# Second layer's FFN: six groups of four blocks by seven products, with the sums of their weights made in HBM by GpSimd's transfers

## The chip, the cores and the metric

One core of a Trainium2 chip runs the whole program. The engines of a core run side by side, each in its own order, and wait for each other through semaphores: TensorE (PE; PEld is its loading of stationary tiles) multiplies, VectorE (DVE) and ScalarE (ACT) work element by element, GpSimd (POOL) does the little that is left, and SyncE (SP) issues the transfers of weights from HBM. The metric is the device time of one execution in microseconds, lower being better; the median of three runs before the change is 2675.32 us.

## What is computed

The program is a decoder trunk of two layers over 256 tokens of width 2048, in float32. The first layer has multi-head latent attention, the second a dilated attention in three groups; behind each stands the same feed-forward network (FFN), whose up-projection has 2 x 5632 columns (a gate half and a value half) and whose down-projection has 5632 rows:

```python
def conv_ffn(h, w_up, conv_w, conv_b, w_down):
    u = h @ w_up
    up = jnp.pad(u, ((0, 0), (CONV_WIDTH - 1, 0), (0, 0)))
    c = conv_b + up[:, 0:S] * conv_w[0]
    for j in range(1, CONV_WIDTH):
        c = c + up[:, j:j + S] * conv_w[j]
    gate, val = c[..., :FFN_HIDDEN], c[..., FFN_HIDDEN:]
    return (jax.nn.silu(gate) * val) @ w_down

for i in range(DEPTH):
    h = rms_norm(x, attn_norm[i])
    ...
    h = rms_norm(x, ffn_norm[i])
    x = x + conv_ffn(h, ffn_w_up[i], ffn_conv_w[i], ffn_conv_b[i], ffn_w_down[i])
return rms_norm(x, final_norm)
```

## The kernel before

**Precision.** A weight tile w that has arrived from HBM is split into a high part wh (ScalarE, the line `nc.scalar.activation(h, w[:, c:e], AF.Copy)` of `load`, L91) and a remainder wl = w - wh (VectorE, L92). The activations are kept as such pairs too (`xs`, `a`). A product is then high by high, high by low and low by high; low by low is left out.

**A unit.** The ordinary product, `proj` (L137), makes one block of 128 output columns for all 256 tokens. The weight block is stationary. For each of the 16 chunks of the 2048 rows, wh meets 512 columns (the tokens' high and low parts side by side) and wl meets 256. An up-projection of one FFN block takes two such units, gate and value (`up`); there are 44 blocks. `keep` then multiplies by the norm's factors (L972), and `conv` does the convolution, the SiLU and the product of the halves (L958 to L967) and leaves the pair `a` for the down-projection. `down` runs 16 chunks of output columns over 10 to 12 finished blocks at a time; the bank of PSUM is first seeded with the residual (L120).

**A four by seven products.** In each layer three groups of four blocks (`SEVEN = (12, 23, 34)`) are done in another way, `seven`: tokens, rows and the two halves gate and value are each cut in two, and seven products take the place of eight, as in Strassen's scheme. Here the tokens' forms are stationary (128 columns) and the weights of four blocks move: each of the seven products has 8 steps of three matmuls of 512 columns (L853 to L855), 168 matmuls for a four. The forms of the tokens (s1 to s4) are made once by `make_forms` (L820 to L827). Four of the seven products need sums of weight blocks, which VectorE makes on the chip from tiles that have arrived (L881, L892, L893) before they are split. When all products are there, `sums` and `last_sum` add them up, `turn` transposes the result back with TensorE (L947, 16 matmuls for a four), and `conv` reads it from PSUM.

**Order.** A scheduler lays out each engine's instructions from the order of the code. Six of a four's products ride between the chunks of a `down` (`mains`), the seventh (`thirds`) and the turns between later units (`steps`). Weights stream through three tiles `w` (pool `wst`) and five tiles each of wh and wl (pool `wsp`), so a load waits until the tile three loads back has been split, and a split until TensorE has used the piece five pieces back. GpSimd's part is small: constants, the zero columns of `upad` (L802) and the reciprocal square roots of the norms (L309), one small instruction at the start of each stage, on which TensorE's instruction that spreads the result (`spread`, L296) waits.

## Time and profile before

| what | value |
|---|---|
| median of three runs (range) | 2675.32 us (2675.04 to 2677.12) |
| span of the profiled execution | 2673.9 us, 1.4 us under that median; the rest lies around the span |
| TensorE's first matmuls of the second FFN | 1938.4 us |
| TensorE's last matmul of the second FFN's last `down` | 2661 us |
| bytes read from HBM | 501.50 MB, 188 GB/s over the span |

In the rows of the profile a line is that of the kernel, an arrow points from what is read to what is written, and x384 counts instructions. In a timeline the first two numbers are the start in the span and the length in microseconds; since matmuls are pipelined, the cost of a run of matmuls is read from the start of the next one, not from the length. A row of a table by windows gives, for a stretch of the span, its length and then how many microseconds of it each engine was busy, the granted clock (1.00 is full), the share of time that the 16 DMA engines were busy, and GB/s.

### The profile page before, as it was taken

To read this page: it belongs to the slowest core of one execution; us is meant where nothing else is said; L and a number is where in the kernel's file an instruction comes from. 1 tells how busy PE (TensorE), PEld (TensorE's weight loads), DVE (VectorE), ACT (ScalarE), POOL (GpSimd) and SP (SyncE) were. 2 spreads that over 40 slices of the span, in tenths; PEclk is the share of its full clock that TensorE was granted. 3 is DMA by queue.
4 is the path that set the end of the run, shared out by engine and by line. 5 is a ranking of instruction groups with operands and counts; after the bars stand their busy time and mean duration, and the time that the engine had idled before them with its cause. 6 is when DMAs were issued, how large, how long until landed. Compare 5 with 4: busy or idle time off the path is not lost.

```text
span 2673.9 us, 40017 instructions
## 1 busy us (share of the span) xinstructions
PE 2657.8 (99%) x15167; PEld 2338.4 (87%) x15167; DVE 2105.5 (79%) x3630; ACT 1639.7 (61%) x2624; POOL 24.7 (1%) x39
## 2 busy tenths in 40 slices
PE   9999999999999999999999999999999999999998
PEld 7998888888888888898888888888888888888887
DVE  7987888898898876676577667667688889889885
ACT  6775666676666764444454444445666667666665
POOL 2000000000000000000000000000000000000000
PEclk9999999999999999999999999999999999999999
DMA  6335555656566565544544544544555575755744
GB/s 246 138 133 203 189 182 193 239 179 224 197 202 227 182 206 198 179 171 170 191 170 164 197 161 174 188 174 160 189 189 175 191 249 171 223 205 189 237 169 147
DMA packets 153553, 506.19 MB, mean 189 GB/s; under 512 B 11024, under 2 KB 86160, under 8 KB 118928
## 3 DMA queue, kind: packets, MB, share of 16 engines
q1 hardware_dynamic: 153072, 503.46, 54.9%
q8 instruction: 119, 1.95, 0.3%
q14 instruction: 74, 0.61, 0.1%
q10 hardware_dynamic: 288, 0.18, 0.0%
HBM read 501.50 MB, written 2.10 MB: 188 GB/s over the span
## 4 chain that ended last, share of the span: by engine, by line
PE 95%; DMA 1%; DVE 1%; issue 0%; ACT 0%; SPq 0%; DVEq 0%; ACTq 0%
PE pp L137 70%; PE pp L165 3%; PE pp L167 3%; PE pp L166 3%; PE ps L855 1%; PE ps L853 1%; PE ps L854 1%; DMA w<-in_wup 1%; PE pp L104 1%; PE pp L106 1%; PE pp L105 1%; PE pp L853 1%; PE pp L854 1%; PE pp L855 1%; PE po L781 1%; PE ps L744 1%
## 5 line engine op out<-in xcount | busy, mean ns | idle before, releaser
L92 DVE TENSOR_TENSOR wl<-w,wh 128x1024 fp32r<-128x1024 f32 (+3 forms) x802 | 881.9, 1110 | 371.0 <-ACT wh L91 228.1
L91 ACT ACTIVATE wh<-w 128x1024 fp32r<-128x1024 f32 (+3 forms) x802 | 770.9, 966 | 370.8 <-PE pp L137 220.7
L137 PE MATMUL pp<-xs,wh 128*128 128x512 f32 x3648 | 855.5, 390 | 0.0
L137 PEld LDWEIGHTS pp<-xs,wh 128*128 128x128 f32 x3648 | 677.1, 188 | 135.8 <-DVE xs L266 0.2
L137 PE MATMUL pp<-xs,wl 128*128 128x256 f32 x3648 | 465.3, 284 | 0.0
L137 PEld LDWEIGHTS pp<-xs,wl 128*128 128x128 f32 x3648 | 455.7, 191 | 9.3
L137 PE MATMUL pp<-a,wh 128*128 128x512 f32 x1920 | 459.7, 390 | 0.0
L137 PEld LDWEIGHTS pp<-a,wh 128*128 128x128 f32 x1920 | 357.7, 188 | 72.6
L137 PEld LDWEIGHTS pp<-a,wl 128*128 128x128 f32 x1920 | 248.1, 191 | 10.2
L137 PE MATMUL pp<-a,wl 128*128 128x256 f32 x1920 | 252.8, 283 | 0.0
L155 DVE TENSOR_TENSOR wl<-w,wh 128x1024 fp32r<-128x1024 f32 x96 | 116.2, 1218 | 62.3 <-ACT wh L154 50.3
L154 ACT ACTIVATE wh<-w 128x1024 fp32r<-128x1024 f32 x96 | 101.6, 1059 | 96.5 <-PE pp L166 50.0
L213 ACT ACTIVATE lo<-pp 128x256 f32<-128x256 f32 x225 | 85.7, 381 | 119.5 <-PE pp L137 119.4
L165 PE MATMUL pp<-wh,xs 128*128 128x512 f32 x384 | 150.0, 391 | 0.0
L167 PE MATMUL pp<-wl,xs 128*128 128x512 f32 x384 | 149.5, 389 | 0.0
L166 PE MATMUL pp<-wh,xs 128*128 128x512 f32 x384 | 149.4, 389 | 0.0
L962 DVE SCALAR_TENSOR_TENSOR cv<-upad,convs,cv 128x256 f32<-128x256 f32 x256 | 121.1, 481 | 18.3 <-ACT cv L958 15.9
L958 ACT ACTIVATE cv<-upad,convs 128x256 f32<-128x256 f32 x128 | 76.4, 598 | 72.7 <-DVE upad L972 71.0
L215 DVE TENSOR_TENSOR sum<-pp,lo 128x256 f32<-128x256 f32 x225 | 94.1, 418 | 0.2
L120 ACT ACTIVATE pp<-x 128x512 f32<-128x512 f32 x144 | 85.1, 591 | 13.6 <-DVE sum L215 6.8
L880 ACT ACTIVATE wh<-w 128x1024 fp32r<-128x1024 f32 x48 | 51.0, 1062 | 60.0 <-PE pp L137 43.0
L167 PEld LDWEIGHTS pp<-wl,xs 128*128 128x128 f32 x384 | 72.1, 188 | 15.0
(299 smaller groups left out, 3154.7 us busy)
## 6 DMA issues: line engine op xcount, KB each, us to landing
w<-in_wup SPq DMA_DIRECT2D x128, 1024.0 KB, 4.8
w<-in_win SPq DMA_DIRECT2D x96, 1024.0 KB, 4.8
w<-in_wup SPq DMA_DIRECT2D x96, 512.0 KB, 5.1
w<-in_win SPq DMA_DIRECT2D x96, 512.0 KB, 4.1
w<-in_wdn SPq DMA_DIRECT2D x64, 704.0 KB, 4.1
w<-in_wdn SPq DMA_DIRECT2D x32, 768.0 KB, 4.2
w<-in_wdn SPq DMA_DIRECT2D x32, 640.0 KB, 5.3
w<-in_wo SPq DMA_DIRECT2D x16, 1024.0 KB, 4.7
```

Source lines behind the costliest of these rows:

```text
L91: nc.scalar.activation(h, w[:, c:e], AF.Copy)
L92: nc.vector.tensor_sub(l, w[:, c:e], h.bitcast(F32))
L120: nc.scalar.activation(dst, chunk.unsqueeze(1).to_broadcast([P, 2, 2, P]), AF.Copy, scale=0.5)
L137: nc.tensor.matmul(ps[:, i * T:], w_k, xs[k][:, :(2 - i) * T], start=(k == 0 and i == own), stop=(k == n - 1), skip_group_check=(i != own))
L154: nc.scalar.activation(wh4, src, AF.Copy)
L155: nc.vector.tensor_sub(wl4, src, wh4.bitcast(F32))
L165: nc.tensor.matmul(ps, xh, wh, start=k == 0, stop=False)
L166: nc.tensor.matmul(ps, xl, wh, start=False, stop=False)
L167: nc.tensor.matmul(ps, xh, wl, start=False, stop=k == KC - 1)
L213: nc.scalar.activation(t, ps[:, T:], AF.Copy)
L215: nc.vector.tensor_add(u, ps[:, :T], t)
L962: nc.vector.scalar_tensor_tensor(o, v, convs[:, cw + j:cw + j + 1], o, op0=ALU.mult, op1=ALU.add)
```

## The change

The first layer keeps its code. The second layer's FFN, now `ffn_ahead`, does six fours by seven products instead of three, and so 20 blocks by ordinary units instead of 32. The sums of weights are no longer made on the chip: `plan_sums` lays out, for each of the six fours, four sums t1 to t4 in HBM, each by a plain copy of a weight block (96 transfers of 512 KB) and transfers that add another block or sum to it in place (96 more). They stand on GpSimd's queue. `some_ahead`, called by every `load` from the ninth on, issues the next copy and the add that is six steps older on two of five loads, and ties both to the last high split that was recorded (`state["split"]`), so that they aren't issued ahead of it. There are 102 steps. The weight of each of the seven products is now loaded as two tiles of 1 MB in rows of 2 KB, from the weights or from the sums, and split like any other. Rows are halved as first half and second half (before: even and odd chunks). The products of a four come one by one (1, 2, 6, 7, 4, 5, 3), each into a bank of pool `pss`, and `use` adds each up as it is done. `PERIODS` and the calls of `deal` and `put` place these half products and the turns behind single units and single chunks of `down`.

```diff
+FIRST = 12
+PERIODS = ((0, 11, 12, 16, (20, 21, 22)), (11, 22, 23, 27, (31, 32, 33)), (22, 33, 34, 38, (42, 43)))
...
+            some_ahead()
...
-                        nc.scalar.activation(h, w[:, c:e], AF.Copy)
+                        state["split"] = nc.scalar.activation(h, w[:, c:e], AF.Copy)
...
+        ahead = []
+        made = {}
+        def plan_sums(layer, fours):
+            copies, adds = [], []
+            for fb0 in fours:
+                t = {i: hbm.tile([4, P, WS], F32, name=f"t{i}_{layer}_{fb0}") for i in (1, 2, 3, 4)}
+                made[layer, fb0] = t
+                last = None
+                for f in range(4):
+                    blk = lambda h, j: wup_d[layer, 2 * (fb0 + f) + h, :, j * WS:(j + 1) * WS]
+                    copies += [(t[i][f], blk(*hj)) for i, hj in ((1, (0, 0)), (3, (1, 1)), (2, (1, 1)), (4, (0, 1)))]
+                    adds += [(t[1][f], blk(1, 0)), (t[3][f], blk(1, 0)), (t[2][f], t[1][f])]
+                    if last:
+                        adds.append(last)
+                    last = (t[4][f], t[2][f])
+                adds.append(last)
+            late = 6
+            for n in range(len(copies) + late):
+                ahead.append((copies[n] if n < len(copies) else None, adds[n - late] if n >= late else None))
+        def some_ahead():
+            state["loads"] = state.get("loads", 0) + 1
+            if state["loads"] > 8 and state["loads"] % 5 in (0, 3) and ahead:
+                c, a = ahead.pop(0)
+                made_by = []
+                if c:
+                    made_by.append(nc.gpsimd.dma_start(*c))
+                if a:
+                    made_by.append(nc.gpsimd.dma_start(*a, accum_op=ALU.add, max_dma_last_dim=WS))
+                for i in made_by:
+                    tc.add_manual_dep(i.ins, state["split"].ins.name, mybir.DependencyInfo(
+                        mybir.DependencyClass.Sync, mybir.DependencyReason.SCHED_ONLY), reason="pace")
...
+        def ffn_ahead(layer, goff, ready):
...
+            products = {1: ("a11", (0, 0)), 2: ("a12", (0, 1)), 3: ("s4", (1, 1)), 4: ("a22", 4), 5: ("s1", 1),
+                        6: ("s2", 2), 7: ("s3", 3)}
+            def seven(fb0):
+                t = made[layer, fb0]
+                ps = {}
+                u = {}
+                quarters = {}
+                def product(i, q):
+                    name, what = products[i]
+                    if q == 0:
+                        ps[i] = pss.tile([P, 512], F32, name="ps", tag="ps")
+                    w = wst.tile([P, D], F32, name="w", tag="w")
+                    if isinstance(what, int):
+                        src = t[what][:, :, q * HALF:(q + 1) * HALF]
+                    else:
+                        h, j = what
+                        src = wup_d[layer, 2 * fb0:2 * fb0 + 8].rearrange("(f i) p c -> i f p c", i=2)[h]
+                        src = src[:, :, j * WS + q * HALF:j * WS + (q + 1) * HALF]
+                    nc.sync.dma_start(w.rearrange("p (f c) -> p f c", f=4), src.rearrange("f p c -> p f c"))
+                    w5 = w.rearrange("p (f k c) -> p k f c", f=4, k=4)
+                    for h in range(2):
+                        wh = wsp.tile([P, WS], F32R, name="wh", tag="wh")
+                        wl = wsp.tile([P, WS], F32R, name="wl", tag="wl")
+                        as4 = lambda t: t.rearrange("p (k f c) -> p k f c", k=2, f=4)
+                        nc.scalar.activation(as4(wh), w5[:, 2 * h:2 * h + 2], AF.Copy)
+                        nc.vector.tensor_sub(as4(wl), w5[:, 2 * h:2 * h + 2], as4(wh).bitcast(F32))
+                        for k in range(2):
+                            kk = 4 * q + 2 * h + k
+                            xh, xl = stationary(name, kk)
+                            bh, bl = wh[:, ts(k, HALF)], wl[:, ts(k, HALF)]
+                            nc.tensor.matmul(ps[i], xh, bh, start=(kk == 0), stop=False)
+                            nc.tensor.matmul(ps[i], xl, bh, start=False, stop=False)
+                            nc.tensor.matmul(ps[i], xh, bl, start=False, stop=(kk == KC // 2 - 1))
+                    if q == 1:
+                        sums.append(lambda: use(i))
...
+                out = []
+                for i in (1, 2, 6, 7, 4, 5, 3):
+                    for q in range(2):
+                        out.append(lambda i=i, q=q: (product(i, q), None if q == 1 else settle()))
+                return out, settle, [lambda f=f: turn(f) for f in range(4)]
...
+            first = [[] for _ in range(2 * FIRST)]
+            downs = [[[] for _ in range(KC)] for _ in PERIODS]
+            ups = [[[] for _ in range(2 * len(p[-1]))] for p in PERIODS]
+            def put(rows, at, *moves):
+                rows[at].extend(moves)
+            def deal(moves, rows, counts):
+                for row, n in zip(rows, counts):
+                    row.extend(moves[:n])
+                    del moves[:n]
+            for s, (a, b, one, two, singles) in enumerate(PERIODS):
+                m, settle, turns = seven(one)
+                if s == 0:
+                    deal(m, first[12:], [1] * 12)
+                    deal(m, downs[0], (1, 1))
+                else:
+                    put(ups[s - 1], 0, m.pop(0))
+                    put(ups[s - 1], 1, m.pop(0))
+                    deal(m, ups[s - 1][4:], (2, 2))
+                    deal(m, downs[s], (2, 2, 2, 2))
+                m, settle2, turns2 = seven(two)
+                put(downs[s], 4, settle, m.pop(0))
+                put(downs[s], 5, m.pop(0))
+                put(downs[s], 6, *turns[:2])
+                put(downs[s], 7, *turns[2:])
+                deal(m, downs[s][8:], (1, 2, 1, 2, 1, 2, 1, 2))
+                ups[s][0].insert(0, settle2)
+                ups[s][2] += turns2[:2]
+                put(ups[s], 3, *turns2[2:3])
+                if len(ups[s]) > 4:
+                    put(ups[s], 4, *turns2[3:])
+                else:
+                    put(ups[s], 3, *turns2[3:])
+            slots = first
+            for fb in range(FIRST):
+                up(fb)
+            for (a, b, _, _, singles), d, u in zip(PERIODS, downs, ups):
+                slots = d
+                down(a, b)
+                slots = u
+                for fb in singles:
+                    up(fb)
+            flush()
+            down(PERIODS[-1][1], FB, True)
+            flush()
...
+        plan_sums(1, [fb for _, _, one, two, _ in PERIODS for fb in (one, two)])
...
-            ffn(1, G_FFN + KC, final)
+            ffn_ahead(1, G_FFN + KC, final)
```

Counted over the program, TensorE loses 384 matmuls of 512 columns and 384 of 256 from its units, and gains 504 of 512 columns in the sevens and 48 transposes.

Three places show how the order stands. First GpSimd's queue, with the reciprocal square roots (`rcol<-ms,negh`; the one of row 20 belongs to the first FFN). Before, only the zeroing of `upad` stood ahead of it:

```order
13 L309 TENSOR_TENSOR rcol<-ms,negh 128x2 [waits DVE_49]
14 L321 TENSOR_TENSOR s_546<-ms,negh 128x2 [waits DVE_49]
15 L321 TENSOR_TENSOR s_759<-ms,negh 128x2 [waits DVE_49]
16 L802 MEMSET upad_3600 128x2 [waits DMAHW6_49,PE_49,Activation_49]
...
20 L309 TENSOR_TENSOR rcol<-ms,negh 128x2 [waits DVE_49] x2
```

Now it stands in the row of transfers. `t_1_12_122` is sum t4 of the four that begins at block 12 (119 to 122 are t1 to t4), a row from `in_wup` at L224 is a copy, a row at L226 an add; the names behind "waits" are semaphores: DMASW of earlier transfers of this queue, Activation of ScalarE, DVE of VectorE.

```order
36 L224 DMA t_1_12_122<-in_wup 128x1024 [waits DMASW0_49,Activation_49]
37 L226 DMA t_1_12_120<-t_1_12_119 512x256 [waits DMASW5_49,DMASW1_49]
38 L224 DMA t_1_12_119<-in_wup 128x1024 [waits DMASW2_49,Activation_49]
39 L226 DMA t_1_12_122<-t_1_12_120 512x256 [waits DMASW3_49]
40 L348 TENSOR_TENSOR rcol<-ms,negh 128x2 [waits DVE_49]
41 L224 DMA t_1_12_121<-in_wup 128x1024 [waits DMASW4_49,Activation_49]
42 L226 DMA t_1_12_119<-in_wup 128x4x256
43 L224 DMA t_1_12_120<-in_wup 128x1024 [waits DMASW6_49,Activation_49]
```

The square root now has four transfers ahead of it that belong to the same few loads, and two of these wait for earlier transfers.

Second, TensorE's rows around the turns of a four that is finished inside a `down` (L961 are the transposes, to the banks `pt` and `po`; L141 with `a` are the chunks of `down`, 11 blocks each; L915 to L917 are the sevens):

```order
9299 L141 MATMUL pp<-a,wh 128x512 x11
9300 L141 MATMUL pp<-a,wl 128x256 x11
9301 L961 MATMUL pt<-cst,t_21020 128x128 x2
9302 L961 MATMUL pt<-cst,t_21019 128x128 x2
9303 L961 MATMUL po<-cst,t_21020 128x128 x2
9304 L961 MATMUL po<-cst,t_21019 128x128 x2
9305 L141 MATMUL pp<-a,wh 128x512 x11
9306 L141 MATMUL pp<-a,wl 128x256 x11
9307 L141 MATMUL pp<-a,wh 128x512 x2
9308 L961 MATMUL pt<-cst,t_21020 128x128 x2
9309 L961 MATMUL pt<-cst,t_21019 128x128 x2
9310 L141 MATMUL pp<-a,wh 128x512 x9
```

Between the first pair of turns and the second stand one chunk and a piece of the next, and the fourth turn follows the first matmul of a seven, two rows below the last one shown. Before, a pair of turns stood inside an ordinary unit (here the second pair of the third four; L137 with `xs`):

```order
10900 L137 MATMUL pp<-xs_19795,wl 128x256
10901 L947 MATMUL pt<-cst,t_25705 128x128 x2
10902 L947 MATMUL pt<-cst,t_25704 128x128 x2
10903 L947 MATMUL po<-cst,t_25705 128x128 x2
10904 L947 MATMUL po<-cst,t_25704 128x128 x2
10905 L137 MATMUL pp<-xs_19041,wl 128x256
```

Two whole units lay between the two pairs, and ordinary units followed the second.

Third, the end of the second FFN. Before, three units stood between the last turn and the last `down`, which began like this (L137 with `a`):

```order
11000 L137 MATMUL pp<-xs_19795,wh 128x512
11001 L137 MATMUL pp<-a,wh 128x512 x11
11002 L137 MATMUL pp<-a,wl 128x256 x22
11003 L137 MATMUL pp<-a,wh 128x512 x12
11004 L137 MATMUL pp<-a,wl 128x256 x2
11005 L137 MATMUL pp<-a,wh 128x512 x13
```

Now the turns stand at the last unit, and the last two lie at and inside the first chunks of the last `down`, which need the blocks that are being turned:

```order
10757 L141 MATMUL pp<-xs_20013,wl 128x256
10758 L961 MATMUL pt<-cst,t_25697 128x128 x2
10759 L961 MATMUL pt<-cst,t_25696 128x128 x2
10760 L141 MATMUL pp<-a,wh 128x512 x5
10761 L141 MATMUL pp<-a,wl 128x256 x6
10762 L141 MATMUL pp<-a,wh 128x512 x6
10763 L961 MATMUL po<-cst,t_25697 128x128 x2
10764 L961 MATMUL po<-cst,t_25696 128x128 x2
10765 L141 MATMUL pp<-a,wh 128x512
10766 L141 MATMUL pp<-a,wl 128x256
10767 L141 MATMUL pp<-a,wh 128x512 x2
10768 L141 MATMUL pp<-a,wl 128x256
```

The three units that lay between are gone, and three chunks instead of two are begun without their last block (`down` of `ffn_ahead`).

130 lines of the change are left out of this document (added).

## Prediction

> **What bounds the kernel now.** The page's totals come first, then its slices, the transfers and the chain of waits.
>
> ```profile
> span 2673.9 us, 40017 instructions
> PE 2657.8 (99%) x15167; PEld 2338.4 (87%) x15167; DVE 2105.5 (79%) x3630; ACT 1639.7 (61%) x2624; POOL 24.7 (1%) x39
> ...
> DMA  6335555656566565544544544544555575755744
> ...
> q1 hardware_dynamic: 153072, 503.46, 54.9%
> ...
> PE 95%; DMA 1%; DVE 1%; issue 0%; ACT 0%; SPq 0%; DVEq 0%; ACTq 0%
> ```
>
> TensorE is busy 99% of the span and makes 95% of the chain. A busy TensorE need not be at its peak, so I look for waits stage by stage, in tables by windows.
>
> ```profile
> core 0: us, PE busy (x) PEld busy (x) DVE busy (x) ACT busy (x) POOL busy (x), PEclk, DMA share, GB/s
> 34.00:1843.00 1809.00, 1807.36 (x10416) 1597.08 (x10415) 1402.47 (x2545) 1060.35 (x1695) 6.53 (x9) 1.00 0.54 186
> 1938.40:2661.00 722.60, 721.88 (x4019) 631.91 (x4018) 613.26 (x945) 492.44 (x776) 1.61 (x1) 1.00 0.58 195
> 488.00:515.00 27.00, 27.00 (x149) 23.62 (x150) 25.65 (x36) 19.14 (x27) 0.00 (x0) 1.00 0.87 292
> 2160.00:2170.00 10.00, 10.00 (x64) 8.81 (x63) 9.66 (x12) 7.61 (x11) 0.00 (x0) 1.00 0.91 310
> 2210.00:2220.00 10.00, 10.00 (x59) 8.80 (x58) 9.37 (x21) 8.56 (x18) 0.00 (x0) 1.00 0.43 163
> 2220.00:2230.00 10.00, 10.00 (x58) 8.73 (x57) 9.99 (x22) 8.16 (x17) 0.00 (x0) 1.00 0.29 105
> 2230.00:2240.00 10.00, 10.00 (x57) 8.73 (x56) 9.73 (x19) 6.35 (x13) 0.00 (x0) 1.00 0.43 136
> 2240.00:2250.00 10.00, 10.00 (x61) 8.93 (x60) 9.96 (x18) 6.76 (x12) 0.00 (x0) 1.00 0.69 218
> ```
>
> Two things are to be seen. Before the second FFN TensorE idles 1.6 us of 1809, in the second FFN 0.7 of 723, both at the full clock: there is no wait to remove, so the change can win only by what TensorE no longer has to do. And TensorE stays full while VectorE is busy 39.1 of 40 us (2210 to 2250) and while the DMA engines are busy 0.87 over 27 us, at 292 GB/s: neither of these loads by itself stops it.
>
> **The change, part by part.** *TensorE's work.* What a matmul costs is read from the starts of runs.
>
> ```profile
> 1957.87 7.44 PE L137 MATMUL pp<-xs,wh 128*128 128x512 f32 x32
> 1965.15 4.00 PE L137 MATMUL pp<-xs,wl 128*128 128x256 f32 x32
> 1968.98 6.31 PE L137 MATMUL pp<-xs,wh 128*128 128x512 f32 x27
> ...
> 2169.88 3.82 PE L137 MATMUL pp<-xs,wh 128*128 128x512 f32 x16
> ...
> 2176.25 3.79 PE L137 MATMUL pp<-xs,wh 128*128 128x512 f32 x16
> ...
> 2206.76 0.60 PE L947 MATMUL pt<-cst,t 128*128 128x128 f32 x4
> 2207.20 0.60 PE L947 MATMUL po<-cst,t 128*128 128x128 f32 x4
> 2207.55 2.15 PE L137 MATMUL pp<-xs,wl 128*128 128x256 f32 x16
> ```
>
> 32 high matmuls take 1965.15 - 1957.87 = 7.28 us, 0.2275 each; 32 low ones 3.83, 0.1197 each; so a unit of 16 and 16 takes 5.56 us. Between the rows at 2169.88 and 2176.25 stand 16 high ones (3.64) and 12 of a seven: 2.73 us, 0.2275 each. Eight transposes take 0.79, 0.099 each. So 384 x (0.2275 + 0.1197) = 133.3 us go, and 504 x 0.2275 + 48 x 0.099 = 114.7 + 4.7 = 119.4 us come. The balance is **-13.9 us**, all on the path, since TensorE is the path.
>
> *VectorE and ScalarE.* The sums on the chip go, the split pieces grow.
>
> ```profile
> L92 DVE TENSOR_TENSOR wl<-w,wh 128x1024 fp32r<-128x1024 f32 x189 | 230.5, 1221 | 42.1 <-ACT wh L91 22.2 <-PE pp L137 18.2
> L881 DVE TENSOR_TENSOR t<-w 128x1024 f32<-128x1024 f32 x24 | 29.4, 1223 | 15.6 <-DMA w<-in_wup 14.2 <-DVE x L373 1.3
> L893 DVE TENSOR_TENSOR t<-t,w 128x512 f32<-128x512 f32 x24 | 16.6, 690 | 0.6
> L892 DVE TENSOR_TENSOR t<-w,t 128x512 f32<-128x512 f32 x24 | 16.5, 686 | 0.2
> L91 ACT ACTIVATE wh<-w 128x1024 fp32r<-128x1024 f32 x188 | 197.8, 1054 | 50.9 <-PE pp L137 19.4 <-PE ps L854 11.2 <-PE pp L854 8.0
> ```
>
> Splits of 1024 columns go up by 36 on either engine: +44 us on VectorE, +38 on ScalarE. VectorE loses 29.4 + 16.6 + 16.5 = 62 us of sums, so that it doesn't become fuller on the whole (613 of 723 us now). None of it is on the path while TensorE is fed, so it costs nothing in the sum; the cover is gone where the turns crowd, for which I take rows of the last turns of before (their transposes start at 2564.66 and 2576.63):
>
> ```profile
> 2566.24 0.47 DVE L962 SCALAR_TENSOR_TENSOR cv<-pt,convs,cv 128x254 f32<-128x254 f32 x1
> ...
> 2579.13 1.22 DVE L92 TENSOR_TENSOR wl<-w,wh 128x1024 fp32r<-128x1024 f32 x1
> 2580.27 0.48 DVE L962 SCALAR_TENSOR_TENSOR cv<-pt,convs,cv 128x254 f32<-128x254 f32 x1
> 2580.68 0.48 DVE L962 SCALAR_TENSOR_TENSOR cv<-po,convs,cv 128x254 f32<-128x254 f32 x1
> ...
> 2581.86 0.41 DVE L967 TENSOR_TENSOR cv<-cv 128x256 f32<-128x256 f32 x1
> 2582.19 1.22 DVE L92 TENSOR_TENSOR wl<-w,wh 128x1024 fp32r<-128x1024 f32 x1
> ```
>
> From start to start a convolution step takes 0.40, a small product 0.33, a split 1.14. A turned block has four steps and two small ones, 2.3 us; four take 9. VectorE begins 1.6 us after the transposes. In the `down` that holds turns, VectorE's rows from there to the splits of the next chunk are 9.0 + 3 residuals (1.0) + 2 splits of 1024 and one of 384 (2.8), done at 14.4 us; TensorE gets there after two chunks of 22 matmuls (7.6), 16 transposes (1.6), half a product (2.7) and the next chunk's high part (2.5), at 14.4. That is even, not behind. There are three such places and two among units; at no wait they cost 0, at 2 us each 10. I take **1 us** for all, by the windows 2210 to 2250, where the same crowd stops nothing.
>
> *The end of the second FFN.* Now TensorE has, from the first pair of turns to the end of the three begun chunks, one unit (5.6), the transposes (1.6) and 33 pairs (11.5): 18.6 us. VectorE's rows up to the last block are 20 steps (8.0), 12 small ones (4.0), a split of 1024 (1.1), two of 384 (1.0), the 1.6 at the start, and some 1.2 of waits for ScalarE: 16.9 us, and behind the last block stand the matmuls that read it and its neighbour, up to 12 pairs (4.2). That is 21, 2.4 late at most. The ends are 0 and 5 (as much again for waits on ScalarE); I take **+2 us**.
>
> *The sums in HBM.* No row shows a transfer from HBM to HBM, nor an add. The q1 row gives 0.549 x 2673.9 / 503.46 = 2.9 us of all 16 engines for a MB, so 1.5 for 512 KB. The upper bound for one is the whole time to landing of such a load:
>
> ```profile
> w<-in_wup SPq DMA_DIRECT2D x128, 1024.0 KB, 4.8
> ...
> w<-in_wup SPq DMA_DIRECT2D x96, 512.0 KB, 5.1
> ```
>
> 192 transfers take 295 us of all engines by the lower bound, 979 by the upper. I take 1.5 for a copy and twice that for an add, which reads two operands: 96 x 4.6 = 440. They are spread over the 1809 us of the second row of windows: a DMA share of 0.54 + 0.24 = 0.78, under the 0.87 at which TensorE stays full. Cost taken: **0**; below nothing it can't go, as TensorE has no wait there. By the upper bound the share would be 1.08, and the time 147 us more. A load lands after 4.8 us and has two units, 11.1 us, so even twice the landing time is covered. The page "DMA: Bandwidth & Descriptors" of the Trainium skill (Issuing engines are not separate DMA queues) speaks against the change: transfers started by GpSimd run on the same 16 engines as SyncE's and interleave with them, so a queue of its own hides nothing. By it the 440 us are taken out of what the loads leave; were the queue free, nothing would be. The trace before has no such transfer and can't tell.
>
> What is queued behind the adds' waits is, on GpSimd, the reciprocal square root of two norms (first FFN, dilated attention). Its row takes 1.6 us, and a wait of the adds before it is for transfers issued two steps, five units or some 28 us, earlier; a miss costs a few us twice. In the second FFN loads grow by 31 MB, from 195 to some 243 GB/s; where two products ride on each chunk, 2.8 MB come in 24 x 0.2275 + 3.8 = 9.3 us, 304 GB/s, beside 310 in the row at 2160, where TensorE is full.
>
> The sum: -13.9 + 1 + 2 + 0 = -10.9, a span of 2663.0. The profiled execution lies 1.4 under the median of 2675.3, so the time is **2664.4 us**.
>
> **Rivals.** (a) *VectorE becomes the bound in the second FFN.* For: the places above are even to within 1 us, and a seven uses up a piece in 1.4 us where a unit takes 2.8, so the five pieces give half the lead. Against: the full windows. With 2 us at each of five places and 5 at the end it is 2673.9 - 13.9 + 15 + 1.4 = 2676: no change. (b) *The sums saturate the DMA engines; slower.* From 0.46 x 1809 = 832 us of free engine time, 96 copies take 147; the rest is 7.1 us for an add. Under that nothing happens, over it each microsecond is 96 us of TensorE's time. At 7.5 us an add the time is 2664 + 0.4 x 96 = 2702. For: adds are unmeasured, in pieces of 1 KB, and read what they write. Against: the threshold is more than twice my price. (c) *Bursts.* Where loads already take 0.87, 27 us in each of three fours of the first layer, two copies and two adds (9.2 us) make 23.5 + 9.2 = 32.7 us of work in 27; 5.7 late, hardly more than the lead of 6.3 us; without that lead, 3 x 5.7 = 17 more, 2681. The same page (Queues, rings and completion order) says that each engine takes turns between queues packet by packet, by which a load's rate may halve beside a sum; that is this case, and nothing before shows it. (d) *The change doesn't do what it says*: the sums aren't done when the second FFN loads them. The last is issued with the 263rd load, near 1840 us, over 170 before the first is read; with a stall of the queue it would be about 2680.
>
> **How the numbers follow.** The forecast has 0.70 (2660 to 2670), (a) 0.12, (b) 0.10, (c) 0.05, (d) 0.03. The range reaches from 2660 (no wait at all, -13.9) to 2681, over (a) and (c), and leaves out (b), most of (d) and a little below. A measurement of this kernel can tell 0.2%, 5.4 us, from no change. Faster takes the forecast and a little of (a): 0.71; same most of (a) and some of (c) and (d): 0.13; slower (b), and the rest: 0.16.
>
> **What would show it.** TensorE's busy time falls by some 14 us, its idle time in windows before 1843 us stays under 3. The second FFN, 722.6 us now, takes some 712. A wait for wl (VectorE) in front of L141 or L915 at the turns, or for `a` in the last `down`, is (a) and the term for the end. A DMA share near 1 in the first 1830 us, with TensorE waiting for wh and ScalarE for transfers, is (b) or (c); loads that land after 5 to 10 us with TensorE full would show the price of the sums right. The prediction is wrong if TensorE's idle time grows by more than 8 us.

## The result, and the profile after

The change made the kernel slower: 2707.89 us median (2700.81 to 2713.5) against 2675.73 us for the kernel before on the same chip, a ratio of 1.012 with a 95% interval of 1.0104 to 1.0136. The profiled execution took 2708.66 us. Its page:

```profile
span 2706.9 us, 39979 instructions
...
PE 2662.2 (98%) x14950; PEld 2323.7 (86%) x14951; DVE 2084.0 (77%) x3568; ACT 1656.2 (61%) x2651; POOL 190.3 (7%) x231
...
q1 hardware_dynamic: 155952, 534.92, 55.7%
q0 software_dynamic: 64512, 100.68, 18.9%
...
PE 85%; DMA 6%; DVE 5%; ACT 2%; issue 2%; POOL 0%; SPq 0%; DVEq 0%; ACTq 0%; POOLq 0%
```

TensorE has 14 us less to do, yet its busy time is 4.4 us longer than before (2657.8) and the span has 44.7 us in which it is idle, 16.1 before. The chain that ended last now holds 6% of DMA. The new queue q0, the sums, takes 0.189 x 2706.9 = 512 us of all 16 engines.

Which stage lost the time is read from one small instruction at the start of each stage, GpSimd's reciprocal square root, in the timelines of its queue. Before (its line is L309):

```profile
272.03 1.61 POOL L309 TENSOR_TENSOR rcol<-ms,negh 128x2 f32<-128x2 f32 x1 [85.06 <-DVE ms L307]
993.99 1.61 POOL L309 TENSOR_TENSOR rcol<-ms,negh 128x2 f32<-128x2 f32 x1 [720.35 <-DVE ms L307]
1944.72 1.61 POOL L309 TENSOR_TENSOR rcol<-ms,negh 128x2 f32<-128x2 f32 x1 [88.75 <-DVE ms L307]
2663.57 0.69 POOL L309 TENSOR_TENSOR rcol<-ms,negh 128x2 f32<-128x2 f32 x1 [717.23 <-DVE ms L307]
```

After (L348):

```profile
273.21 1.64 POOL L348 TENSOR_TENSOR rcol<-ms,negh 128x2 f32<-128x2 f32 x1 [5.00 <-DVE ms L346]
1028.24 1.64 POOL L348 TENSOR_TENSOR rcol<-ms,negh 128x2 f32<-128x2 f32 x1 [4.99 <-DVE ms L346]
1978.98 1.64 POOL L348 TENSOR_TENSOR rcol<-ms,negh 128x2 f32<-128x2 f32 x1 [88.77 <-DVE ms L346]
2696.70 0.68 POOL L348 TENSOR_TENSOR rcol<-ms,negh 128x2 f32<-128x2 f32 x1 [716.08 <-DVE ms L346]
```

From start to start: up to the first FFN +1.2 us, the **first FFN 722.0 to 755.0, +33.1**, the dilated attention 950.7 both times, the **second FFN 718.9 to 717.7, -1.1**. So two questions stand: why the stage whose code did not change lost 33 us, and why the one that changed won 1 and not 11. The windows by these stages, after:

```profile
270.20:1025.20 755.00, 732.93 (x4020) 632.17 (x4018) 619.81 (x963) 486.81 (x780) 89.60 (x103) 1.00 0.89 264
1025.20:1976.00 950.80, 950.74 (x5319) 833.51 (x5320) 648.56 (x1181) 469.42 (x649) 63.71 (x75) 1.00 0.71 217
1976.00:2693.70 717.70, 710.18 (x3784) 612.50 (x3784) 590.98 (x879) 515.95 (x798) 1.64 (x1) 0.99 0.70 240
```

At a DMA share of 0.71 the attention idles for 0.1 us; at 0.89 the first FFN idles for 22.1. Within the first FFN, cut where a unit's convolution starts, before:

```profile
280.50:403.30 122.80, 122.80 (x712) 108.91 (x711) 106.61 (x188) 82.83 (x133) 0.00 (x0) 1.00 0.53 184
403.30:515.90 112.60, 112.60 (x596) 96.69 (x595) 99.90 (x137) 75.59 (x113) 0.00 (x0) 1.00 0.65 218
515.90:577.40 61.50, 61.50 (x360) 54.58 (x359) 56.11 (x103) 43.27 (x76) 0.00 (x0) 1.00 0.53 180
```

and after:

```profile
281.70:405.40 123.70, 123.70 (x717) 109.68 (x716) 106.58 (x188) 82.55 (x133) 15.42 (x18) 1.00 0.87 259
405.40:536.90 131.50, 119.22 (x597) 98.71 (x596) 99.81 (x136) 75.34 (x113) 14.02 (x16) 0.97 0.83 244
536.90:599.20 62.30, 62.30 (x365) 55.31 (x364) 56.07 (x103) 42.33 (x76) 6.92 (x8) 1.00 0.87 256
```

The second row of each is the `down` in which a four's products ride: 18.9 us longer, with 12.3 us of idle time, while the units beside it lose 1.7 together at a *higher* share, 0.87 against 0.83. The other two such stretches (578.3 to 693.1 and 757.3 to 872.0 before) lose 9.9 and 6.8 us, at shares of 0.90 and 0.92. What lies behind each of these two takes 2.0 and 2.2 us less than before, with fewer matmuls between the same marks (365 in place of 373, 672 in place of 685); with that the parts add up to the 33.1. VectorE and ScalarE are busy for no longer in the first FFN than before (619.8 and 486.8 us, 622.4 and 496.2 before), so their work did not get slower. One stall of the first stretch, after, in the timelines of SyncE's queue, GpSimd, VectorE and TensorE:

```profile
428.72 0.94 SPq L1160 DMA_DIRECT2D w<-in_wup  x2
429.76 4.06 SPq L82 DMA_DIRECT2D w<-in_wdn  x2
445.38 0.93 SPq L1160 DMA_DIRECT2D w<-in_wup  x2
...
427.18 0.55 POOL L224 DMA_DIRECT2D t<-in_wup  x1 [16.41 <-ACT wh L95]
427.71 1.31 POOL L226 DMA_DIRECT2D t<-in_wup  x1
...
439.37 1.23 DVE L1168 TENSOR_TENSOR t<-w 128x1024 f32<-128x1024 f32 x1 [5.32 <-DMA w<-in_wup]
...
439.03 0.50 PE L1140 MATMUL ps<-wh,xs 128*128 128x512 f32 x1 [1.11 <-ACT wh L1167]
439.36 0.40 PE L1141 MATMUL ps<-wh,xs 128*128 128x512 f32 x1
442.12 0.50 PE L1142 MATMUL ps<-wl,xs 128*128 128x512 f32 x1 [2.36 <-DVE wl L1170]
442.45 0.54 PE L1140 MATMUL ps<-wh,xs 128*128 128x512 f32 x1
442.79 0.63 PE L1141 MATMUL ps<-wh,xs 128*128 128x512 f32 x1
443.21 0.63 PE L1142 MATMUL ps<-wl,xs 128*128 128x512 f32 x1
```

It reads so. A copy and an add go out at 427.2 and 427.7. The 1 MB for the four's next rows, two transfers of 512 KB, is issued at 428.7 and is there at 439.4: 10.6 us, where such transfers land after 4.7 us in the same stretch of before (median of 12). VectorE waits 5.3 us for it, and TensorE 1.1 us for ScalarE's split and 2.4 us for VectorE's. Then the clock falls: from 442.8 the matmuls of 512 columns start 0.43 us apart, 0.2275 at the full clock, and between 443 and 446 the granted clock is 0.51. The Trainium skill ("TensorE: Matmul & The Clock Gate", Part 1) has the array at half rate after an idle window of about 3.4 us; the trace roughly agrees, with 3.5 us of idle time here out of 4.2. The next load of the four goes out 16.7 us behind this one; before, two such loads went out 11.6 us apart:

```profile
437.89 0.93 SPq L873 DMA_DIRECT2D w<-in_wup  x2
...
449.52 0.94 SPq L873 DMA_DIRECT2D w<-in_wup  x2
```

At the other end, the second FFN's last turns, after, TensorE's timeline, and a row of the windows:

```profile
2627.83 0.73 PE L141 MATMUL pp<-a,wh 128*128 128x512 f32 x2 [0.23 <-DVE a L392]
2631.76 0.58 PE L141 MATMUL pp<-a,wl 128*128 128x256 f32 x1 [3.20 <-ACT a L391]
...
2634.59 1.22 PE L141 MATMUL pp<-a,wh 128*128 128x512 f32 x2 [1.15 <-ACT wh L95]
```

```profile
2630.00:2640.00 10.00, 7.09 (x22) 5.62 (x23) 5.71 (x15) 3.99 (x8) 0.00 (x0) 0.52 0.22 72
```

The begun chunks wait 4.6 us for the last blocks `a` and the splits behind them, and the granted clock is 0.52 in the ten microseconds around it, so that by an estimate from these two numbers some 3.4 of the 7.1 us in which TensorE is busy there are the clock's. The row of 3.2 us names ScalarE, the last to write that `a`; ScalarE itself had waited 1.39 us for VectorE just before (at 2630.99).

### The profile page after: what moved, and what is told of

It reads as the page before. It is cut to its first block, busy times and chain, and to the rows that moved or that the text cites. A ratio compares the mean times of both kernels' runs of the same rounds, so it can differ in the third digit from the quotient of the medians.

```text
span 2706.9 us, 39979 instructions
## 1 busy us (share of the span) xinstructions
PE 2662.2 (98%) x14950; PEld 2323.7 (86%) x14951; DVE 2084.0 (77%) x3568; ACT 1656.2 (61%) x2651; POOL 190.3 (7%) x231
## 3 DMA queue, kind: packets, MB, share of 16 engines
q0 software_dynamic: 64512, 100.68, 18.9%
## 4 chain that ended last, share of the span: by engine, by line
PE 85%; DMA 6%; DVE 5%; ACT 2%; issue 2%; POOL 0%; SPq 0%; DVEq 0%; ACTq 0%; POOLq 0%
PE pp L141 59%; DMA w<-in_wup 4%; PE pp L169 3%; PE pp L171 3%; PE pp L170 3%; PE ps L915 2%; PE ps L916 2%; PE ps L917 2%; DVE wl L96 2%; PE pp L108 1%; PE pp L110 1%; PE pp L109 1%; DMA w<-t 1%; DVE wl L910 1%; ACT wh L95 1%
## 5 line engine op out<-in xcount | busy, mean ns | idle before, releaser
L96 DVE TENSOR_TENSOR wl<-w,wh 128x1024 fp32r<-128x1024 f32 x754 | 821.7, 1103 | 340.9 <-ACT wh L95 230.5
L95 ACT ACTIVATE wh<-w 128x1024 fp32r<-128x1024 f32 x754 | 717.5, 959 | 355.5 <-PE pp L141 184.9
L141 PE MATMUL pp<-xs,wh 128*128 128x512 f32 x3264 | 767.8, 390 | 1.9 <-ACT wh L95 1.3
L141 PEld LDWEIGHTS pp<-xs,wh 128*128 128x128 f32 x3264 | 606.0, 188 | 124.4 <-ACT wh L95 1.7
L141 PE MATMUL pp<-a,wh 128*128 128x512 f32 x1920 | 464.6, 392 | 1.4 <-ACT wh L95 1.1
L141 PE MATMUL pp<-xs,wl 128*128 128x256 f32 x3264 | 421.4, 285 | 6.5 <-DVE t L1198 3.5
L141 PEld LDWEIGHTS pp<-xs,wl 128*128 128x128 f32 x3264 | 411.5, 192 | 17.1 <-DVE wl L96 4.3
L141 PEld LDWEIGHTS pp<-a,wh 128*128 128x128 f32 x1920 | 357.8, 189 | 74.4 <-ACT wh L95 1.9
L141 PEld LDWEIGHTS pp<-a,wl 128*128 128x128 f32 x1920 | 249.7, 192 | 17.1 <-ACT a L391 4.0
L141 PE MATMUL pp<-a,wl 128*128 128x256 f32 x1920 | 255.4, 284 | 4.6 <-ACT a L391 3.2
L910 DVE TENSOR_TENSOR wl<-w,wh 128x1024 fp32r<-128x1024 f32 x168 | 201.8, 1221 | 41.4 <-ACT wh L909 39.5
L909 ACT ACTIVATE wh<-w 128x1024 fp32r<-128x1024 f32 x168 | 172.9, 1056 | 73.9 <-DMA w<-t 32.5
L159 DVE TENSOR_TENSOR wl<-w,wh 128x1024 fp32r<-128x1024 f32 x96 | 116.2, 1218 | 62.3 <-ACT wh L158 50.3
L158 ACT ACTIVATE wh<-w 128x1024 fp32r<-128x1024 f32 x96 | 101.7, 1059 | 97.9 <-PE pp L170 49.9
L224 POOL DMA_DIRECT2D t<-in_wup x96 | 52.1, 543 | 1509.5 <-ACT wh L95 1354.7
L252 ACT ACTIVATE lo<-pp 128x256 f32<-128x256 f32 x201 | 76.3, 379 | 89.2 <-PE pp L141 88.9
L254 DVE TENSOR_TENSOR sum<-pp,lo 128x256 f32<-128x256 f32 x201 | 84.0, 418 | 2.4 <-ACT lo L252 2.3
```

What stands on the lines that cost most here:

```text
L95: state["split"] = nc.scalar.activation(h, w[:, c:e], AF.Copy)
L96: nc.vector.tensor_sub(l, w[:, c:e], h.bitcast(F32))
L141: nc.tensor.matmul(ps[:, i * T:], w_k, xs[k][:, :(2 - i) * T], start=(k == 0 and i == own), stop=(k == n - 1), skip_group_check=(i != own))
L158: nc.scalar.activation(wh4, src, AF.Copy)
L159: nc.vector.tensor_sub(wl4, src, wh4.bitcast(F32))
L254: nc.vector.tensor_add(u, ps[:, :T], t)
```

## The experiments

Stages are from the norms' instructions, as above; "first FFN" was 722.0 before and 755.0 after, "second FFN" 718.9 and 717.7. Ratios are against the kernel before on the same chip, with the 95% interval.

| run | median us | ratio | first FFN | second FFN |
|---|---|---|---|---|
| e1 sums alone | 2708.45 | 1.0124 (1.0109 to 1.0140) | 753.1 | 718.1 |
| e2 no sums | 2679.41 | 1.0016 (1.0006 to 1.0025) | 722.5 | 718.5 |
| e3 not beside the fours | 2678.50 | 1.0013 (1.0003 to 1.0022) | 723.2 | 719.6 |
| e4 copies "in 1 KB" | 2703.99 | 1.0114 (1.0094 to 1.0133) | 752.9 | 717.8 |
| e5 destination in 1 KB rows | 2709.78 | 1.0125 (1.0110 to 1.0140) | 757.9 | 718.6 |
| e6 copies for adds | 2690.81 | 1.0062 (1.0045 to 1.0079) | 732.9 | 718.5 |
| e9 two copies for an add | 2727.36 | 1.0192 (1.0177 to 1.0208) | 775.2 | 718.1 |
| e13 one at a time | 2704.49 | 1.0113 (1.0099 to 1.0127) | 750.5 | 718.2 |
| e14 source in 1 KB rows | 2801.51 | 1.0478 (1.0462 to 1.0494) | 830.2 | 728.8 |
| e16 four load buffers | 2676.89 | 1.0009 (0.9998 to 1.0019) | 721.5 | 717.6 |
| e17 the same with sums | 2697.51 | 1.0079 (1.0061 to 1.0097) | 745.0 | 717.6 |
| e18 half beside the fours | 2685.23 | 1.0036 (1.0024 to 1.0049) | 731.5 | 718.3 |
| e7 turns earlier | 2676.23 | 1.0004 (0.9995 to 1.0014) | 723.0 | 714.4 |
| e8 turns apart | 2670.12 | 0.9984 (0.9974 to 0.9994) | 725.3 | 709.1 |
| e11 mostly in the attention | 2667.87 | 0.9974 (0.9964 to 0.9984) | 725.2 | 713.9 |
| e12 turns apart, no sums | 2671.18 | 0.9984 (0.9976 to 0.9993) | 722.8 | 713.2 |
| e15 last four earlier | 2668.66 | 0.9978 (0.9969 to 0.9987) | 726.2 | 710.8 |

**Which half of the change costs the time.** *e1*, the change with the old second FFN:

```diff
-            ffn_ahead(1, G_FFN + KC, final)
+            ffn(1, G_FFN + KC, final)
```

> The kernel before, with the sums' transfers alone: they are made, nobody reads them, and the second FFN is that of before. In the changed kernel the time from the first FFN's norm to the next norm grew from 722.0 to 755.0 us, the first attention by 1.2, the dilated attention by 0.0, and the second FFN shrank by 1.1. Theory (the sums' transfers delay the weight loads of the first layer's fours): all of the 34 us are here too, so about 2709 us, with TensorE idle some 20 us more between 400 and 930 us and the first FFN's stage at 755. Rival (the forecast: the transfers cost nothing, and the time went with something else, such as the order of the loads): 2675 us.

All of the loss is there, with nobody reading a sum: the first FFN takes 1025.02 - 271.96 = 753.1 us.

```profile
271.96 1.64 POOL L348 TENSOR_TENSOR rcol<-ms,negh 128x2 f32<-128x2 f32 x1 [5.00 <-DVE ms L346]
1025.02 1.64 POOL L348 TENSOR_TENSOR rcol<-ms,negh 128x2 f32<-128x2 f32 x1 [4.62 <-DVE ms L346]
```

The forecast's zero is out.

*e2*, the new second FFN without sums:

```diff
-        plan_sums(1, [fb for _, _, one, two, _ in PERIODS for fb in (one, two)])
...
-                    if isinstance(what, int):
-                        src = t[what][:, :, q * HALF:(q + 1) * HALF]
+                    h, j = plain[what] if isinstance(what, int) else what
```

> The changed kernel without the sums' transfers: its second FFN loads plain blocks of the weights where it loaded sums (the same bytes in the same pieces), so its output is another. Theory: the first FFN's stage is 722 us again, and the second FFN's is 717.7 as in the changed kernel, -1.1 against before: 2674 us. By the forecast's own terms for the second FFN (-13.9 + 1 + 2) it would be 2664. If the sums' late arrival or their queue held up the second FFN too, it lies between these two.

The first FFN is back at 722.5. The second does not win alone either: 718.5. Its TensorE is busy less, but idles 7.2 us (0.7 before), and its clock is low around 2590 to 2610.

*e3*, no step beside the first layer's fours, more elsewhere:

```diff
-            if state["loads"] > 8 and state["loads"] % 5 in (0, 3) and ahead:
+            if state["loads"] > 8 and state["loads"] % 2 == 0 and ahead and not state.get("four"):
...
+                    state["four"] = True
                     down(seg)
```

> The changed kernel, with no sum's transfer issued while the first layer's fours run (three stretches of some 110 to 130 us), and every second load elsewhere in place of two in five, so that as many transfers are spread over 1570 us in place of 1908. Theory (the transfers hurt only beside the fours' loads, whose pieces are small): the first FFN's stage is 722 to 725 us, the others as in the changed kernel, 2675 to 2679 us in all. Rival (the amount of transfers in all decides, wherever they are put): the loss of 33 us moves to other stages, 2700 or more.

As many transfers in all cost 1 us in the first FFN and none in the attention, whose DMA share is now 0.80.

```profile
272.08 1.64 POOL L348 TENSOR_TENSOR rcol<-ms,negh 128x2 f32<-128x2 f32 x1 [4.98 <-DVE ms L346]
995.26 1.64 POOL L348 TENSOR_TENSOR rcol<-ms,negh 128x2 f32<-128x2 f32 x1 [4.38 <-DVE ms L346]
```

So the place is settled: beside the fours.

**What it is about a transfer that costs time there.** *e4* and *e5* meant to make the copies' pieces smaller.

```diff
-                    made_by.append(nc.gpsimd.dma_start(*c))
+                    made_by.append(nc.gpsimd.dma_start(*c, max_dma_last_dim=T))
```

> The changed kernel, with its 96 copies in pieces of 1 KB in place of 4 KB; the adds are as they were. In the first layer's fours SyncE's queue moves 24.3 MB in 13485 packets, 1.8 KB each. Theory A (the engines take turns packet by packet, so that a load in pieces of 1 KB gets a fifth of the bytes beside a copy in pieces of 4 KB): with equal pieces it gets half, and the 33 us of the first FFN fall to 15 to 22, 2690 to 2697 us in all. Theory B (what counts is the engine time that the transfers take): a copy in small pieces takes no less time than the 1.8 us of now and at most the 3.7 us of an add, so the loss stays or grows, 2708 to 2725 us.

```diff
-                t = {i: hbm.tile([4, P, WS], F32, ...) for i in (1, 2, 3, 4)}
+                t = {i: hbm.tile([4, 4, P, T], F32, ...) for i in (1, 2, 3, 4)}
+                t = {i: h.rearrange("f a p c -> f p a c") for i, h in t.items()}
```

> The kernel before with the sums' transfers alone, where the sums lie in HBM in rows of 1 KB in place of 4 KB, so that a copy can't move more than 1 KB in one piece (its 512 KB then make some 528 packets, as an add's do, in place of 144). With rows of 4 KB that kernel took 2708.5 us, its first FFN's stage 753.1 in place of 722.0. Theory A (the engines take turns between queues packet by packet, and the fours' loads, in pieces of 1 KB, get a fifth of the bytes beside a copy in 4 KB): with equal pieces they get half; the stage falls to 735 to 742, the time to 2690 to 2697. Theory B (the engine time of the transfers counts): smaller pieces take as much time or more, the stage is 753 or longer, the time 2708 to 2725.

Neither did: both profiles show 64512 packets on q0, as in the changed kernel. They tell nothing of the packets; as near repeats they show by how much the stage can differ from run to run, 753 to 758.

*e6* and *e9* change what stands beside a copy: each add becomes one plain copy (e6) or two (e9). The price of each kind comes from the two ends of the changed kernel's sums, where six transfers of one kind stand alone: copies between 70 and 181 us,

```profile
q0 software_dynamic: 864, 3.15, 9.8%
```

and adds between 1766 and 1890:

```profile
q0 software_dynamic: 3168, 3.15, 18.1%
```

0.098 x 111 / 6 = 1.8 us of all engines and 144 packets for a copy, 0.181 x 124 / 6 = 3.7 us and 528 packets for an add.

```diff
-                    made_by.append(nc.gpsimd.dma_start(*a, accum_op=ALU.add, max_dma_last_dim=WS))
+                    made_by.append(nc.gpsimd.dma_start(*a))
```

> The kernel before with the sums' transfers alone, and each of the 96 adds is a plain copy of the same source to the same place (so that no sum is made; nothing reads them). By packets and shares a copy takes 1.8 us of all 16 engines, an add 3.7. Theory A (turns: pieces of 4 KB hurt, the adds' pieces of 1 KB hardly): twice as many copies hurt as much or more; the first FFN's stage is 753 to 785, the time 2708 to 2740. Theory B (engine time): 192 x 1.8 = 346 us in place of 533, so the loss of 31 us falls by a third or more, since it comes only where the load is past what fits: stage 742 or less, 2697 or less.

```diff
-                    made_by.append(nc.gpsimd.dma_start(*a, accum_op=ALU.add, max_dma_last_dim=WS))
+                    made_by.append(nc.gpsimd.dma_start(spare[state["loads"] % 4], a[1]))
+                    made_by.append(nc.gpsimd.dma_start(*a))
```

> The kernel before with the sums' transfers alone, and each of the 96 adds as two plain copies of its source, one to its place and one to a spare place (no sum is made; nothing reads them). With adds the first FFN's stage took 753.1 us (31 more than before), with one copy for each add 732.9 (11 more). Three copies take 3 x 1.8 = 5.4 us of all 16 engines, a copy and an add 1.8 + 3.7 = 5.5, but the add's 528 packets become 288. Theory B (the engine time of the transfers counts): the stage is 748 to 757, the time 2704 to 2713. Rival (an add is worse than its engine time, by its many small packets or by the reading of what it writes): 740 or less, 2696 or less.

*e14* writes each source as four blocks of 1 KB rows, and the sums' tiles likewise:

```diff
-                t = {i: hbm.tile([4, P, WS], F32, ...) for i in (1, 2, 3, 4)}
+                t = {i: hbm.tile([4, 4, P, T], F32, ...) for i in (1, 2, 3, 4)}
...
-                    blk = lambda h, j: wup_d[layer, 2 * (fb0 + f) + h, :, j * WS:(j + 1) * WS]
+                    blk = lambda h, j: wup_d[layer, 2 * (fb0 + f) + h, :, j * WS:(j + 1) * WS].rearrange("p (a c) -> a p c", c=T)
```

> The kernel before with the sums' transfers alone, each source written as four blocks of 128 rows of 1 KB, one block behind the other, so that the source of a copy can't be one run of 4 KB. Its packets (144 a copy up to now, whatever the destination's rows) show whether that makes smaller ones: 64512 in all would mean that it doesn't, and that the run tells nothing new. If it does: theory A (the engines take turns packet by packet, so a load gets less beside larger packets): the first FFN's stage falls from 753.1 to 735 to 742, the time to 2690 to 2697. Rival (the packets' size doesn't matter, or smaller ones take longer): 753 or more, 2708 or more.

Here the packets did change, to 175104, and by more than the copies'. Between 70 and 181 us, where six copies stand alone, each makes 3168 / 6 = 528 packets, in the same engine time as before (0.089 x 111 / 6 = 1.6 us), and lands after 10.4 us, where it took 5.2:

```profile
q0 software_dynamic: 3168, 3.18, 8.9%
```

If the 48 adds of one sum to another kept their 528 packets, which no row shows alone, the 48 adds from the weights made 2064 each, pieces of 256 B: 144 x 528 + 48 x 2064 = 175104. So e14 changes two kinds of transfers, and does not say which of them cost the time. The views of the transfers between 405 and 530 us show the sums' queue (packets, MB, share) and the landing time of the down projection's loads. Before the change, then sums alone (e1), copies for adds (e6), two copies for an add (e9), 1 KB rows (e14):

```profile
w<-in_wdn SPq DMA_DIRECT2D x12, 640.0 KB, 5.5
```

```profile
q0 software_dynamic: 4704, 7.34, 29.9%
w<-in_wdn SPq DMA_DIRECT2D x12, 640.0 KB, 7.0
```

```profile
q0 software_dynamic: 1968, 8.39, 21.5%
...
w<-in_wdn SPq DMA_DIRECT2D x13, 640.0 KB, 7.1
```

```profile
q0 software_dynamic: 2352, 11.01, 28.5%
w<-in_wdn SPq DMA_DIRECT2D x12, 640.0 KB, 8.9
```

```profile
q0 software_dynamic: 12922, 6.57, 28.0%
w<-in_wdn SPq DMA_DIRECT2D x14, 640.0 KB, 10.2
```

e6 alone looked as if the engine time decided: two thirds of it, a third of the loss. e9 and e14 say no. At shares of 28.0 to 29.9% the first FFN lost 31 (e1), 53 (e9) and 108 us (e14). Nor is it the size of the packets in either direction: fewer, larger ones cost more in e9 (which moves half as many bytes again), many small ones far more in e14. With e1, e9 and e14 the down loads' landing time rises in the order of the losses: 7.0, 8.9, 10.2 us; two runs do not fit in, e6 with 7.1 us and a third of e1's loss, and e13, below, with 8.1 us and a loss of 28.5.

*e13* issues the same transfers one at a time, each behind a load of its own:

```diff
-            if state["loads"] > 8 and state["loads"] % 5 in (0, 3) and ahead:
+            if state["loads"] > 9 and state["loads"] % 5 in (0, 3, 1, 4) and ahead:
```

> The kernel before with the sums' transfers alone, as many in the same time, but each behind a load of its own: a copy behind the first and fourth load of five, an add behind the second and fifth, in place of both at once behind two. With both at once the first FFN's stage is 753.1 us, 31 more than before. Theory (what hurts is that transfers issued at once stand beside the same load: each takes its turns, and the load is later than its lead): the loss is less than half, stage 737 or less, 2692 or less. Rival (the bytes moved over the stretch count, however they are dealt out): 750 to 757, 2706 to 2713.

About a tenth of the loss went. *e18* halves the steps beside the fours:

```diff
+            if ... and (state["loads"] % 5 == 0 or state["loads"] % 5 == 3 and not state.get("half")) and ahead:
```

> The kernel before with the sums' transfers alone, and beside the first layer's fours one step in five loads in place of two; elsewhere as in the changed kernel. Theory (the mean demand counts: loads take 0.65 of the engines' time in those stretches, a step of 5.5 us in each 14.6 us makes 1.03, in each 29 us 0.84): the first FFN's stage is 722 to 727 us, in place of 753, and the time 2675 to 2681. Rival (each step delays the load beside it, whatever the mean): half of the 31 us, a stage of 734 to 741, 2688 to 2696.

Neither: 9.5 us, between the 0 to 5 of a threshold and the 15 of a fixed price per step. None, half and all of the steps cost 1, 10 and 31 us, which is more than in proportion.

*e16* and *e17* give the loads one more buffer, without and with sums:

```diff
-        wst = ctx.enter_context(tc.tile_pool(name="wst", bufs=3))
-        wsp = ctx.enter_context(tc.tile_pool(name="wsp", bufs=5))
+        wst = ctx.enter_context(tc.tile_pool(name="wst", bufs=4))
+        wsp = ctx.enter_context(tc.tile_pool(name="wsp", bufs=4))
```

> The kernel before with four load buffers in place of three, and four pairs of split pieces in place of five (the space of the one goes to the other). It is the control for the next: TensorE was full before, so about 2675 us, or some us more if four pairs of pieces are too few.

> The same with the sums' transfers. With three buffers they made the first FFN's stage 31 us longer. Theory (the loads of the fours land 2 to 5 us later beside sums, and three buffers give them no more lead than before): with a fourth buffer, one more load of lead, the stage grows by 12 us or less against the kernel of the control. Rival (the stretch has more to move than it has time for, whatever the lead): it grows by 25 or more.

The stage grows by 23.5 in place of 31, between the theory's 12 and the rival's 25: a lead that is too short is a part of the loss, a quarter by the profiles, more than a third by the medians (20.6 us above the control, where e1 is 33.2 above the kernel before). A lead longer by more than one buffer wasn't tried.

**The second FFN.** *e7* moves the last four's turns one unit earlier, on top of e3; *e8* also deals out the other turns:

```diff
-                    put(ups[s], 3, *turns2[3:])
+                    put(ups[s], 1, *turns2[:2])
+                    put(ups[s], 2, *turns2[2:])
```

> The kernel without sums beside the first layer's fours (2678.5 us), with the four turns of the second FFN's last four one unit earlier each (behind the second and third of the last four units in place of the third and last). In that kernel TensorE idles 4.8 us between 2590 and 2610 and its granted clock is 0.66 for the 10 us behind that. Theory (the turns stand too close to the end, so that VectorE and ScalarE are late with the blocks that the begun chunks read, and the idle time draws the clock down after it): both go, -8 us, 2670 to 2671. Rival (the crowd is set by all the work of the last units, wherever the turns stand): 2676 to 2679.

```diff
-                put(downs[s], 6, *turns[:2])
-                put(downs[s], 7, *turns[2:])
+                for i in range(4):
+                    put(downs[s], 5 + i, turns[i])
```

> As the kernel with the earlier turns, and the turns of the first four of each period one behind each of four chunks of the down projection in place of two behind each of two. In the kernel without sums beside the fours TensorE idles 5.2 us in four places between 2280 and 2510, where such turns or their neighbours stand. Theory (VectorE is late where two turns come at once): most of that goes, another -3 to -5 us, 2666 to 2668. Rival (these waits are for something else, or a turn more in the next chunk delays the next product's sums): no change or up to +3 against the kernel with the earlier turns.

e7's median is only 2.3 us under e3's, in the rival's range and with overlapping intervals; in its profile, of 4.9 us idle time at the end 2.7 stay. e8 is another 6.1 us faster, more than the 3 to 5 expected of it, and the first whose interval lies below 1. The waits it was to remove are those of transposes, in the changed kernel between 2340 and 2545 us:

```profile
PE pt L961 <- ACT wh L909: 2.4, 2, 1.5
```

The row names a split of ScalarE, which no transpose reads. They are the transposes of a third turn, which write the bank `pt` that the first turn filled a chunk earlier. In the first of the two places VectorE's last row of the first turn's convolution, which reads `pt`, ends at 2358.97, the named split at 2359.02, and the transposes start at 2359.12. That they wait for the bank is what the kernel's order suggests; the times do not tell the two apart. With one turn to a chunk the waits are gone from the profile; between 2280 and 2590 TensorE idles 0.3 us. The second FFN there:

```profile
1944.50:2653.60 709.10, 706.03 (x3786) 610.41 (x3785) 589.95 (x879) 517.03 (x798) 1.64 (x1) 1.00 0.71 243
```

*e11* lets the sums stand mostly in the two attentions, *e12* takes them out:

```diff
-            if state["loads"] > 8 and state["loads"] % 2 == 0 and ahead and not state.get("four"):
+            if state["loads"] > 8 and (state["loads"] % 4 == 0 if state.get("ffn") else state["loads"] % 3 != 0) and ahead and not state.get("four"):
```

> The kernel with its turns apart (2670.1 us; first FFN's stage 725.3, second FFN's 709.1 in its profile), with the sums' pace by stage: behind every fourth load in the first FFN outside the fours, behind two loads of three in the two attentions, so that some 67 of 102 steps stand in the dilated attention (a DMA share of about 0.51 + 67 x 5.5 / 951 = 0.90 there). Theory (a transfer costs nothing where what is there leaves its engine time free): first FFN 722 to 723.5, dilated attention 950.7, 2667 to 2668 us in all. Rival (at 0.90 the attention's loads come late too): the dilated attention grows by 3 us or more, 2670 or more.

> The kernel with its turns apart, without the sums' transfers: its second FFN loads plain blocks of the weights where it loaded sums (the same bytes in the same pieces), so its output is another. Theory (what is left of the gain is the second FFN's 709.1 against 718.9, and the sums cost the rest): the first FFN's stage is 722.0, the second FFN's 709, 2665 to 2666 us. Rival (the second FFN is held up by its own loads and waits, so that the profile of the turns apart was a lucky one): 2668 or more.

e11 is **2667.87 us, 0.9974 of the kernel before, the best median of all**: 0.26% less than the kernel before, 0.16 to 0.36% by the interval. GpSimd's instruction between its first FFN and its attention comes some 3 us later in TensorE's stream (4039 matmuls of the first FFN stand ahead of it, 4020 before), so the 725.2 and the 948.2 go together: 0.7 us more than before for both, at a DMA share of 0.84 in the attention. e12, without sums, is no faster, 2671.18 where 2665 to 2666 was expected, and its second FFN took 713.2: its rival holds, by which e8's 709.1 was a lucky profile. So sums in the right place cost nothing that can be measured, and what varies is the second FFN, 709 to 714 us in single profiles.

*e15*, on top of e11, finishes the last four two chunks sooner:

```diff
+                if s == 2:
+                    deal(m, downs[s][8:], (2, 2, 2, 2, 2, 2))
+                    put(downs[s], 14, settle2)
+                    put(downs[s], 15, turns2[0])
```

> The kernel with the sums mostly in the attention (2667.9 us), with the second FFN's last four done two chunks sooner (two products with each of six chunks in place of one and two in turn), its turns one at a time behind the last chunk and the first three of the last four units. In its profile TensorE idles 3.7 us between 2580 and 2620. Theory (VectorE, busy without a break for some 20 us there, has too much in the last units): most of that and of the clock drawn down after it goes, -3 to -5 us, 2663 to 2665. Rival (two products with each of six chunks wait for their loads or for VectorE, which gives it back): 2667 to 2670.

No change against e11 that the medians show. Idle time at the end fell from 3.7 to 1.1 us, while the waits between 2290 and 2480 grew from 2.1 to 2.6.

## Why the prediction was wrong

**TensorE's balance, -13.9: about right.** In e8, where little waiting is left, its busy time in the second FFN is 706.0 in place of 718.2, -12.2; in e7, e11 and e15 it is 707 to 708.

**The sums, 0: the step that failed; they cost 33.1 us in the first FFN.** The sign that the prediction named came, TensorE's idle time grew by 28.6 us, over its 8. The sums' price was nearly right (1.5 and 3.1 us forecast, 1.8 and 3.7 measured; 440 and 512 us in all). The error was to spread it over 1809 us and hold the mean of 0.78 against the 0.87 at which TensorE had been seen full. That row came from loads of one queue; it says nothing about loads that share the engines with another queue. And the mean hid the place: the attention loses nothing at 0.80 and 0.84, the units beside the first four under 1 us each at 0.87, while that four loses 19 us at 0.83. Summed up over this four alone, by the measured prices, the demand is 0.65 + 5.5 / 14.6 = 1.03 (a step for every 2.5 loads of the down projection, one of which goes out each 5.85 us), so the same sum taken by stretch would have shown it full. By that excess alone it would be late by 3 of its 112.6 us, not by 19, and at half the steps, 0.84, the stage still lost 9.5 (e18). The forecast gave a load "two units, 11.1 us" of lead. That holds for units. In the fours two loads of the down projection and one of 1 MB share each 11.7 us; TensorE ran dry 9.2 us after the one above was issued, the splits have to fit into that too, and the load took 10.6.

**Rival (c), 0.05: the right place, too small.** It had the first layer's fours, but only the 27 us of each in which the loads already take 0.87, and 5.7 us for each; it called this hardly more than the lead of 6.3, and it is less. The loss runs over all of their 112 to 115 us, at 0.65 to 0.68, and is 19, 10 and 7 us. It left out that waits also lower the clock behind them: the first FFN's 4020 matmuls are busy for 732.9 us in place of 722.0. Rival (b) did not happen: an add is far under 7.1 us. Nor did (d): the last add went out at 1867 us, the first sum is loaded at 2063. The rule of the Trainium skill cited there ("DMA: Bandwidth & Descriptors", Queues, rings and completion order) has each engine take turns between queues packet by packet. If the profile's packets are those of the rule, a load should get more beside smaller packets; e14 went the other way.

**The end of the second FFN, +2 (0 to 5): too small, 8.8.** The working had VectorE done 2.4 us late at most. It left VectorE's waits for ScalarE at 1.2 us, where four rows between 2617 and 2637 show 2.7 (1.05, 0.67, 0.52 and 0.48), and it added the rows of the two engines as if they ran beside each other, where at the end each waits for the other in turn. And it left the clock at nothing, where TensorE's busy time (710.2, 706.0 in e8) points to 4.2; 4.6 are idle.

**The turns' crowds, +1 (0 to 10): 2.2,** and mostly of another kind: TensorE idles 2.9 us there, less the 0.7 of the whole second FFN before; transposes take 2.4, waiting for the bank or for ScalarE, and products 0.5 for VectorE. The working had counted VectorE's rows against TensorE's, and no bank that has to come free.

The sum: -12.2 for TensorE's work, +2.2, +8.8 and +33.1 for the sums makes +31.9 (the first three add up to the second FFN's -1.2 by the way they are split, with e8's busy time as the measure); with the 1.2 us ahead of the first FFN, which e1 does not show, it is the +33.0 of the span.

**What stays open.** Why equal engine time on the second queue delays the loads by so different amounts (e1, e9, e14), why the landing times of e6 and e13 do not go with their losses, and why the first four loses twice as much as the other two. The runs show the place, the rise with the number of steps, a quarter or more for the lead, and that neither engine time nor simultaneous issue alone sets the amount; fewer, larger packets (e9) and more, smaller ones (e14) both cost more, but each with another change beside it.
